# Elementwise work moved from GpSimd to VectorE and ScalarE, and 1024-column modulation products, in a kernel of two transformer blocks

## The chip, the cores and the metric

One core of a Trainium2 chip runs the whole program. The metric is the device time of one execution in microseconds (us): the median of three runs of the kernel before is 2305.88 us. In the profile PE is TensorE's matmul, PEld its weight load, DVE is VectorE, ACT ScalarE, POOL GpSimd and SP SyncE, whose queue issues nearly all DMAs.

## What is computed

Two networks of two layers each are run one after the other on x, 256 tokens by 1024 features, all in float32. The first is a pre-norm block, the second is modulated by rows that come from a condition c (`w_ada`):

```
for l in range(DEPTH):                       # first block
    h = rmsnorm(x, ffn1_pre_g[l])
    x = x + 0.5 * rmsnorm(swiglu(h, ...), ffn1_post_g[l])
    m = hybrid_mixer(rmsnorm(x, mix_pre_g[l]), w_in[l], w_out[l], ...)
    ...
for l in range(DEPTH):                       # second block
    mod = silu(c) @ w_ada[l] + b_ada[l]      # 1024 x 9216, split in nine rows sh, sc, g
    y = _swiglu(_modulate(x, sh1, sc1), ...)
    x = _post_norm(x, y, g1, FFN_RES, ln_gain[l, 0], ln_bias[l, 0])
    y = _token_mixer(_modulate(x, sh2, sc2), w_in[l], w_out[l])
    ...
```

Each layer is a feed-forward net (inner width 2816), a mixer and a second feed-forward net. The mixer of the first block has four parts (gated delta-net, differential attention, state-space, mLSTM), that of the second three (retention, dilated attention, stick-breaking). Several parts end with a norm over each head: `rmsnorm(o, norm_g)`.

## The kernel before, in words

**Weights.** All products run in TensorE's fast float32 format, with three products per pair to keep precision: each weight is split into a high part H, its rounded copy, and a low part L, the rest. The method `unit` (line 768) does it for 128 x 1024 elements: SyncE loads a raw buffer (tiles `raw`, or `rawx` in the SBUF cells R and S), ScalarE casts it to H (`wH`), and L = raw - H is one subtraction (`wL`). Line 783 chooses the engine of the subtraction: of the units counted in `nunit`, every 5th in a feed-forward net (`POOL_FFN`) and every 2nd elsewhere (`POOL_MIX`) goes to GpSimd, the others to VectorE. Some units of a feed-forward net have other buffers, which the profile names by their cells (X, A). The raw buffer comes free when the subtraction has read it. A feed-forward net has 70 units, the first block's mixer 38, the second's 32.

**Stages.** `ffn` (line 919) streams gate and up units through TensorE in column blocks of 512, applies silu on ScalarE, and splits the product into H and L (tiles A and B); `down` (line 995) streams the down weights into accumulators `pa` and `pb`. Then `post_rms` or `post_ln` norms each half of the tokens (`t` is 0 or 1), and the next stage's `pre_rms` or `modulate` norms, scales and transposes the rows (tiles `h` and G, `tr`, `hT`). The reciprocal root of each norm is a power on GpSimd (`pow_rs`, line 763). The mixers weave the projections (`pj`) with the parts' own small products (`pg`, `po`).

**Modulation rows.** `ada_pieces` (line 1036) is a generator: `unit` draws pieces of it at 0.58 per unit while a feed-forward net runs, from the first block's first net to the second block's first. A piece loads two blocks of 128 weight rows by 512 columns and adds them, times the condition's column, into `aacc` (one buffer of 512 columns). After four pieces the sum over partitions is left to do: `aacc` is split into `aaH` and `aaL`, and `ada_row` (line 1064), two pieces later, multiplies them by ones on TensorE, adds the bias and stores the row.

**Head norms.** `head_norm` (line 1132) squares its rows by a product of the tile with itself, on GpSimd unless told otherwise, then reduces on VectorE.

**Order.** Every operation is recorded, not issued; so nearly all have line 637 in the profile, and groups are told apart by tiles. `Program.emit` (line 516) then gives each tile its place (`rooms`: SBUF cells A, B, X, R, S, G, E, L of set widths, E being 568 columns that only mixer tiles use), links operations that share data, and places them by rank on one timeline per engine and one for the wire, each at a duration that `taken` (line 564) estimates. The program is emitted in the order of the planned starts, so each engine works through its own queue in that order. For GpSimd the estimate is

```
occ = 0.05 + (0.0023 if len(ins) > 1 else 0.0011) * n
```

with n columns, and no term for other engines' work.

Of the kernel before, what the change touches and what calls it, by code (L numbers as in the profile page):

```python
# [12 lines left out]
F32 = mybir.dt.float32  # L13
F32R = mybir.dt.float32r
AF = mybir.ActivationFunctionType
ALU = mybir.AluOpType
# [4 lines left out]
P = 128  # L21
D = 1024
S = 256
DFF = 2816
KD = D // P
# [9 lines left out]
NRL = 4  # L35
NLOC = 2
KA = 12
POOL_FFN = 5
POOL_MIX = 2
STAG = 6  # L40
LAST = 2
AHEAD = 12.0
# [2 lines left out]
HALVES = [slice(0, 512), slice(512, 1024)]  # L45
# [550 lines left out]

CELLS = {"A": 6144, "B": 5120, "X": 4096, "R": 2048, "S": 2048, "G": 1536, "E": 568, "L": 4992}
ROOMS = {F32: ("G", "E", "R", "S", "A", "B"), F32R: ("X",)}  # L600
row = lambda c, n, size=1024, at=0: [(c, at + i * size) for i in range(n)]
PLANS = {
    "ffn": {"aA": row("A", 1), "aB": row("B", 1), "wLx": row("X", 2), "wHx": row("X", 2, at=2048),
# [75 lines left out]
class Kern:  # L679
    def __init__(self, ctx, tc, a, out):  # L680
        self.ctx, self.tc, self.a, self.out = ctx, tc, a, out
        self.clock = Clock()
        self.prog = Program(tc)
        self.nc = Engines(self.prog, self.clock)
        self.last_table = None
        self.nffn = 0
        self.done, self.local, self.table_end = [], None, 0.0
        self.nraw, self.nunit, self.ada_gen, self.ada_rate, self.ada_due = 0, 0, iter(()), 0.0, 0.0

    nbufs = {"pa": 4, "pb": 2, "pj": 2, "pg": 2, "po": 2, "tr": 2}  # L690

# [76 lines left out]
    def unit(self, src, a, n):  # L768

        nc, w = self.nc, a * n  # L770
        where = next(self.local) if self.local else ""
        raw = self.raw()
        if where == "a":
            H, L = next(self.late)
        else:
            pool, nb = (self.lp, NLOC) if where else (self.wp, NW)
            L = self.tl(pool, [P, UNIT], "wL" + where, F32R, bufs=nb)
            H = self.tl(pool, [P, UNIT], "wH" + where, F32R, bufs=nb)
        v = lambda t: t[:, :w].rearrange("p (a n) -> p a n", a=a)
        nc.sync.dma_start(v(raw), src.rearrange("(a p) n -> p a n", p=P))  # L780
        nc.scalar.copy(H[:, :w], raw[:, :w])
        self.nunit += 1
        pooled = self.nunit % (POOL_FFN if self.local else POOL_MIX) == 0
        self.sub(L[:, :w], raw[:, :w], H[:, :w].bitcast(F32), nc.gpsimd if pooled else nc.vector)
        if self.local and ADA_FROM <= next(self.count) < ADA_TO:
            self.ada_due += self.ada_rate
        while self.ada_due >= 1:
            self.ada_due -= 1
            next(self.ada_gen, None)
        return v(H), v(L)  # L790
# [244 lines left out]

    def ada_pieces(self):

        nc, last = self.nc, None
        for l in range(LAYERS):
            for j in range(18):  # L1040
                c0 = j * 512
                acc = self.tl(self.adap, [P, 512], "aacc")
                for k0 in range(0, KD, 2):
                    rv = self.raw().rearrange("p (a n) -> p a n", a=2)
                    nc.sync.dma_start(rv, self.a["w_ada_2"][l, k0 * P:(k0 + 2) * P, c0:c0 + 512]
                                      .rearrange("(a p) n -> p a n", p=P))
                    for k in (k0, k0 + 1):
                        cc = self.cond[:, k:k + 1]
                        if k == 0:
                            self.ts(acc, rv[:, 0], cc, None, ALU.mult)  # L1050
                        else:
                            self.stt(acc, rv[:, k - k0], cc, acc, ALU.mult, ALU.add)
                    if k0 == 2 and last:
                        self.ada_row(*last)
                    if k0 + 2 < KD:
                        yield
                H, L = (self.tl(self.adap, [P, 512], n, F32R) for n in ("aaH", "aaL"))
                nc.scalar.copy(H, acc)
                self.sub(L, acc, H.bitcast(F32))
                last = (l, j, H, L)  # L1060
                yield
        self.ada_row(*last)

    def ada_row(self, l, j, H, L):
        nc, c0, m = self.nc, j * 512, j // 2
        row = self.tl(self.adap, [1, 512], "arow", bufs=1)
        nc.sync.dma_start(row, self.a["b_ada_2"][l:l + 1, c0:c0 + 512])
        ps = self.tl(self.trp, [P, 512], "tr")
        self.mm(ps[0:1], self.onesr, H, True, False)
        self.mm(ps[0:1], self.onesr, L, False, True)  # L1070
        self.add(row, row, ps[0:1])
        if m % 3 == 1:
            self.ts(row, row, 1.0, None, ALU.add)
        elif m % 3 == 2:
            self.ts(row, row, 1.0, 1.0 if m == 5 else 0.5, ALU.add, ALU.mult)
        nc.sync.dma_start(self.mods[l, c0:c0 + 512].unsqueeze(0), row)
        self.mods_done = l * 18 + j + 1
# [51 lines left out]
        self.sub(o[:, :, 0], o[:, :, 0], tmp[:, :, 1])  # L1129
        self.add(o[:, :, 1], o[:, :, 1], tmp[:, :, 0])  # L1130

    def head_norm(self, pool, o, n, w, gate, out, tag, eng=None):

        g = lambda ap: ap.rearrange("p (n w) -> p n w", n=n)
        sq = self.tl(pool, [P, n * w], "nsq", bufs=2)
        ss = self.tl(self.sm, [P, n], tag + "ss", bufs=2)
        self.mul(sq, o, o, eng or self.nc.gpsimd)
        self.nc.vector.tensor_reduce(ss, g(sq), AX.X, ALU.add)
        self.ts(ss, ss, 1.0 / w, EPS, ALU.mult, ALU.add)
        self.pow_rs(ss, ss)  # L1140
        if gate is None:
            self.mul(g(out), g(o), self.bc(ss, w))
            return
        self.mul(g(sq), g(o), self.bc(ss, w))
        self.mul(out, sq, gate)
# [288 lines left out]
    def gdn(self, l, m, GP, trp, T, r4, r8):  # L1434
        nc = self.nc
        V, A, G = nc.vector, nc.scalar, nc.gpsimd
        sp = self.sp1[l]
# [3 lines left out]
        E = {}  # L1441
# [191 lines left out]
        def end():  # L1633
            for t in range(2):
                yield f"gscan{t}"
                o = E["o", t]
                self.head_norm(m, o, 4, 64, None, o, "gn", V if t else G)
                self.mul(r4(o), r4(o), self.bm(sp["gdn_norm_g"], 4))
                yield 0.0
            for t in range(2):  # L1640
                yield f"gg{t}"
                self.mul(E["o", t], E["o", t], T["zg", t][:, 256:512])
                self.out_T(E["o", t], 0, t)
# [3 lines left out]
    def diff(self, l, m, OP, trp, T, r4):  # L1647
        nc = self.nc
        V, A, G = nc.vector, nc.scalar, nc.gpsimd
        sp = self.sp1[l]  # L1650
# [9 lines left out]
        for t in range(2):  # L1660
# [41 lines left out]
            o = tl([P, 256], "ho", 8)  # L1702
            A.copy(o, ps[:, 0:256])
            self.head_norm(m, o, 4, 64, None, o, "dn")
            self.mul(r4(o), r4(o), self.bm(sp["diff_norm_g"], 4), G)
            self.out_T(o, 2, t)
        self.flag("diff")

# [303 lines left out]
    def block2(self):  # L2012
        a = self.a
        with ExitStack() as ctx:
            cp = self.pool("con2p", 1, ctx)
            self.rows = self.pool("rows2", 5, ctx)
            self.con2 = self.tl(cp, [P, C2_ARR.shape[1]], "con2")
            self.nc.scalar.dma_start(self.con2, a["con2"])
            self.ada_rate = ADA_RATE
            steps = [(w, l, j) for l in range(LAYERS) for j, w in enumerate(("ffn1", "mix", "ffn2"))]  # L2020
            for (what, l, j), nxt in zip(steps, steps[1:] + [None]):
                r = {}

                def rows():
                    r["g"] = self.mod_row(l, 3 * j + 2)
                    r["gain"], r["bias"] = (self.rowb(a[n][l, j]) for n in ("ln_gain_2", "ln_bias_2"))
                    if nxt is not None:

                        r["scale"], r["shift"] = (self.mod_row(nxt[1], 3 * nxt[2] + q) for q in (1, 0))
                        b = self.tl(self.sc, [P, D], "h")  # L2030
                        self.mul(b, r["bias"], r["scale"], self.nc.gpsimd)
                        self.add(r["shift"], r["shift"], b, self.nc.gpsimd)
                        self.mul(r["scale"], r["scale"], r["gain"], self.nc.gpsimd)

                def tail(t, acc, trp):
                    yield from self.post_ln(t, acc, r, trp)

                if what == "mix":
                    self.mixer2(l, rows, tail)
                else:  # L2040
                    self.ffn(a[what + "_w_gate_2"][l], a[what + "_w_up_2"][l], a[what + "_w_down_2"][l], rows, tail, NRL - 2)
# [181 lines left out]
    def stick(self, m, GP, T, r4):  # L2223
# [16 lines left out]
        yield from self.scores_T(GP, T["sT"], each)  # L2240
        mk = self.bm(self.c2("mlt"), 4)
        for s in range(2):
            self.mul(sp[s][:, :, 0:P], sp[s][:, :, 0:P], mk, G if s else V)
        yield 0.0
        for s in range(2):
            for t in range(s, 2):
# [6 lines left out]
                yield 0.0  # L2253
        for s in range(2):
            self.act(zs[s], zs[s], AF.Exp)
            self.mul(zs[s][:, :, 0:P], zs[s][:, :, 0:P], mk, G if s else V)
        yield "sv1"
        yield 0.0
        for t in range(2):
# [63 lines left out]
```

## Time and profile before

| | us |
|---|---|
| runs shown | 2313.62, 2301.46, 2305.88 |
| median | 2305.88 |
| profiled execution | 2308.43 |
| its span in the profile | 2306.7 |

The profiled execution lies 2.5 us over the median; 1.7 us of it lie around the span. The feed-forward nets and mixers follow each other. In the profile the first mixer lies from about 210 to 430 us, the second from 830 to 1060, the second block's two from 1457 to 1597 and from 1974 to 2116; the rest are the eight feed-forward nets, of 180 to 210 us each. Busy time counts an instruction from its start to its end, whatever it does in between. A wait is idle time of an engine, put down to what ended it.

### The profile page before, as it was taken

The numbers are of one execution on the slowest core, as the hardware profiler recorded it, in microseconds if no ns is written. First come the engines' busy times: TensorE is split into PE (matmuls) and PEld (weight loads), VectorE is DVE, ScalarE is ACT, GpSimd is POOL, SyncE is SP. The second block draws the span as 40 slices with busy tenths as digits, with TensorE's granted clock in tenths as the row PEclk, the third lists the DMA queues.
The fourth block names the chain that finished last, engine by engine and source line by source line (L and its number), as shares of the span: only waits on it lengthen the run. The fifth ranks groups of instructions, "written<-read, shape, count | busy, mean of one in ns | idle before, by whom it ended". The sixth has DMA issues, their size and how long they took to land.

```text
span 2306.7 us, 36694 instructions
## 1 busy us (share of the span) xinstructions
PE 2180.5 (95%) x14604; PEld 1935.7 (84%) x14604; DVE 1641.6 (71%) x2232; ACT 1003.0 (43%) x1420; POOL 570.6 (25%) x292
## 2 busy tenths in 40 slices
PE   8998999999899989999998999998999999998998
PEld 6986888799689868888986898876998898876996
DVE  6788797787788878877777785757645645757544
ACT  5443443544343445335433445343443445344441
POOL 1212323211121232232111132334311222333211
PEclk9999999999899989999999999999999999999999
DMA  9877422687777854136776767436755656435652
GB/s 321 267 268 224 131 74 82 226 278 243 250 255 252 272 182 129 56 127 228 256 253 233 259 213 242 153 119 194 227 191 179 208 155 227 145 111 197 209 189 72
DMA packets 226747, 455.32 MB, mean 197 GB/s; under 512 B 20808, under 2 KB 56008, under 8 KB 226576
## 3 DMA queue, kind: packets, MB, share of 16 engines
q1 hardware_dynamic: 226288, 451.87, 60.2%
q8 instruction: 114, 1.87, 0.3%
q10 hardware_dynamic: 288, 1.11, 0.1%
q14 instruction: 57, 0.47, 0.1%
HBM read 451.80 MB, written 1.12 MB: 196 GB/s over the span
## 4 chain that ended last, share of the span: by engine, by line
PE 62%; DVE 19%; DMA 9%; issue 6%; ACT 3%; POOL 1%; SPq 0%; DVEq 0%; ACTq 0%; POOLq 0%
PE pa L637 38%; PE pj L637 9%; PE pb L637 5%; PE pg L637 4%; DVE aacc L637 4%; PE po L637 3%; DVE wL L637 3%; DVE A L637 3%; PE tr L637 2%; DVE B L637 2%; DVE G L637 2%; DMA raw<-in_ffn_w_down_dram 1%; DMA raw<-in_ffn_w_up_dram 1%; DVE h L637 1%; DVE X L637 1%
## 5 line engine op out<-in xcount | busy, mean ns | idle before, releaser
L637 PE MATMUL pa<-hT,wH 128*128 128x256 f32 x3008 | 546.5, 283 | 0.0
L637 ACT CAST wH<-raw 128x1024 fp32r<-128x1024 f32 (+2 forms) x374 | 375.4, 1013 | 392.2 <-PE pa L637 141.2
L637 POOL TENSOR_TENSOR wL<-raw,wH 128x1024 fp32r<-128x1024 f32 (+1 forms) x120 | 307.6, 2563 | 702.5 <-ACT wH L637 649.9
L637 PEld LDWEIGHTS pa<-hT,wH 128*128 128x128 f32 x3008 | 469.3, 191 | 2.9 <-issue 1.7
L637 DVE TENSOR_TENSOR wL<-raw,wH 128x1024 fp32r<-128x1024 f32 (+2 forms) x254 | 329.4, 1300 | 173.4 <-ACT wH L637 173.2
L637 PE MATMUL pa<-hT,wL 128*128 128x256 f32 x1504 | 425.8, 283 | 0.0
L637 PE MATMUL pa<-hT,X 128*128 128x256 f32 x2400 | 298.7, 279 | 4.2 <-ACT X L637 3.1
L637 PEld LDWEIGHTS pa<-hT,X 128*128 128x128 f32 x2400 | 288.2, 190 | 6.8 <-ACT X L637 3.3
L637 PEld LDWEIGHTS pa<-hT,wL 128*128 128x128 f32 x1504 | 288.2, 192 | 0.0
L637 PE MATMUL pj<-wH,hT 128*128 128x256 f32 (+1 forms) x768 | 207.0, 348 | 0.5 <-ACT hT L637 0.5
L637 PEld LDWEIGHTS pj<-wH,hT 128*128 128x128 f32 x768 | 137.4, 198 | 21.8 <-issue 4.1
L637 DVE TENSOR_TENSOR wL<-R,wH 128x1024 fp32r<-128x1024 f32 (+1 forms) x88 | 113.2, 1289 | 57.3 <-ACT wH L637 57.2
L637 PE MATMUL pa<-wH,hT 128*128 128x512 f32 x384 | 137.4, 417 | 9.9 <-ACT wH L637 4.5
L637 ACT CAST wH<-R 128x1024 fp32r<-128x1024 f32 (+1 forms) x102 | 100.8, 992 | 92.4 <-PE pa L637 39.0
L637 ACT CAST X<-raw 128x1024 fp32r<-128x1024 f32 (+1 forms) x100 | 98.5, 986 | 93.7 <-PE pa L637 56.5
L637 DVE TENSOR_TENSOR X<-raw,X 128x1024 fp32r<-128x1024 f32 (+1 forms) x77 | 96.1, 1248 | 58.1 <-ACT X L637 57.7
L637 POOL TENSOR_TENSOR X<-raw,X 128x1024 fp32r<-128x1024 f32 (+1 forms) x23 | 57.1, 2485 | 323.3 <-ACT X L637 266.1
L637 PE MATMUL pj<-hT,wH 128*128 128x256 f32 (+1 forms) x672 | 131.3, 295 | 0.0
L637 PE MATMUL pj<-wL,hT 128*128 128x256 f32 (+1 forms) x384 | 129.5, 337 | 0.7 <-POOL wL L637 0.5
L637 DVE SCALAR_TENSOR_TENSOR aacc<-raw,cols,aacc 128x512 f32<-128x512 f32 x132 | 115.3, 873 | 12.2 <-DMA raw<-in_w_ada_dram 9.4
L637 PEld LDWEIGHTS pj<-hT,wH 128*128 128x128 f32 (+1 forms) x672 | 105.6, 192 | 3.8 <-issue 0.7
L637 PE MATMUL pb<-wH,A 128*128 128x512 f32 x288 | 103.0, 399 | 1.5 <-ACT wH L637 1.5
(402 smaller groups left out, 3977.7 us busy)
## 6 DMA issues: line engine op xcount, KB each, us to landing
raw<-in_ffn_w_gate_dram SPq DMA_DIRECT2D x111, 512.0 KB
raw<-in_ffn_w_down_dram SPq DMA_DIRECT2D x110, 512.0 KB
raw<-in_w_in_dram SPq DMA_DIRECT2D x108, 512.0 KB
raw<-in_ffn_w_up_dram SPq DMA_DIRECT2D x86, 512.0 KB
raw<-in_w_ada_dram SPq DMA_DIRECT2D x76, 512.0 KB
R<-in_ffn_w_up_dram SPq DMA_DIRECT2D x57, 512.0 KB
R<-in_ffn_w_down_dram SPq DMA_DIRECT2D x48, 512.0 KB
R<-in_w_ada_dram SPq DMA_DIRECT2D x40, 512.0 KB
```

Of the source, the lines that this page charges most:

```text
L637: getattr(self.prog.tc.nc, self.eng).__getattribute__(name)(*[real(x) for x in a], **{q: real(x) for q, x in k.items()})
```

## The change

Subtractions of weights go to VectorE, all of them. So do the product with `diff_norm_g`, the scale and shift rows of the second block (`rows` in `block2`), and the mask products of `stick`. The squares of `head_norm` go to ScalarE. Modulation products take 1024 columns and one block of 128 weight rows per load; `aacc` has 1024 columns and is split in two halves, one after the other. The cell E is dropped. The powers of `pow_rs` and some memsets stay on GpSimd.

```diff
-POOL_FFN = 5
-POOL_MIX = 2
...
-CELLS = {"A": 6144, "B": 5120, "X": 4096, "R": 2048, "S": 2048, "G": 1536, "E": 568, "L": 4992}
-ROOMS = {F32: ("G", "E", "R", "S", "A", "B"), F32R: ("X",)}
+CELLS = {"A": 6144, "B": 5120, "X": 4096, "R": 2048, "S": 2048, "G": 1536, "L": 4992}
+ROOMS = {F32: ("G", "R", "S", "A", "B"), F32R: ("X",)}
...
         nc.scalar.copy(H[:, :w], raw[:, :w])
-        self.nunit += 1
-        pooled = self.nunit % (POOL_FFN if self.local else POOL_MIX) == 0
-        self.sub(L[:, :w], raw[:, :w], H[:, :w].bitcast(F32), nc.gpsimd if pooled else nc.vector)
+        self.sub(L[:, :w], raw[:, :w], H[:, :w].bitcast(F32))
...
-            for j in range(18):
-                c0 = j * 512
-                acc = self.tl(self.adap, [P, 512], "aacc")
-                for k0 in range(0, KD, 2):
-                    rv = self.raw().rearrange("p (a n) -> p a n", a=2)
-                    nc.sync.dma_start(rv, self.a["w_ada_2"][l, k0 * P:(k0 + 2) * P, c0:c0 + 512]
-                                      .rearrange("(a p) n -> p a n", p=P))
-                    for k in (k0, k0 + 1):
-                        cc = self.cond[:, k:k + 1]
...
-                    if k0 == 2 and last:
-                        self.ada_row(*last)
-                    if k0 + 2 < KD:
+            for m in range(9):
+                acc = self.tl(self.adap, [P, D], "aacc")
+                for k in range(KD):
+                    rv = self.raw()
+                    nc.sync.dma_start(rv, self.a["w_ada_2"][l, k * P:(k + 1) * P, m * D:(m + 1) * D])
+                    cc = self.cond[:, k:k + 1]
+                    if k == 0:
+                        self.ts(acc, rv, cc, None, ALU.mult)
+                    else:
+                        self.stt(acc, rv, cc, acc, ALU.mult, ALU.add)
+                    if k == 3 and last:
+                        self.ada_row(*last.pop())
+                    if k < KD - 1:
                         yield
...
+                for n, c in enumerate(HALVES):
+                    if last:
+                        self.ada_row(*last.pop())
+                    H, L = (self.tl(self.adap, [P, 512], q, F32R) for q in ("aaH", "aaL"))
+                    nc.scalar.copy(H, acc[:, c])
+                    self.sub(L, acc[:, c], H.bitcast(F32))
+                    last.append((l, 2 * m + n, H, L))
                 yield
...
-    def head_norm(self, pool, o, n, w, gate, out, tag, eng=None):
+    def head_norm(self, pool, o, n, w, gate, out, tag):
...
-        self.mul(sq, o, o, eng or self.nc.gpsimd)
+        self.nc.scalar.activation(sq, o, AF.Square)
...
-                self.head_norm(m, o, 4, 64, None, o, "gn", V if t else G)
+                self.head_norm(m, o, 4, 64, None, o, "gn")
...
-            self.mul(r4(o), r4(o), self.bm(sp["diff_norm_g"], 4), G)
+            self.mul(r4(o), r4(o), self.bm(sp["diff_norm_g"], 4))
...
-                        self.mul(b, r["bias"], r["scale"], self.nc.gpsimd)
-                        self.add(r["shift"], r["shift"], b, self.nc.gpsimd)
-                        self.mul(r["scale"], r["scale"], r["gain"], self.nc.gpsimd)
+                        self.mul(b, r["bias"], r["scale"])
+                        self.add(r["shift"], r["shift"], b)
+                        self.mul(r["scale"], r["scale"], r["gain"])
...
-            self.mul(sp[s][:, :, 0:P], sp[s][:, :, 0:P], mk, G if s else V)
+            self.mul(sp[s][:, :, 0:P], sp[s][:, :, 0:P], mk)
...
-            self.mul(zs[s][:, :, 0:P], zs[s][:, :, 0:P], mk, G if s else V)
+            self.mul(zs[s][:, :, 0:P], zs[s][:, :, 0:P], mk)
```

## Rows read from the trace of the kernel before

**Rows 1.** The page, part 1: busy us (share of the span) xinstructions of each engine.

```profile
PE 2180.5 (95%) x14604; PEld 1935.7 (84%) x14604; DVE 1641.6 (71%) x2232; ACT 1003.0 (43%) x1420; POOL 570.6 (25%) x292
```

**Rows 2.** Windows: stretch, length, busy us (x) of PE, PEld, DVE, ACT, POOL, clock, DMA.

```profile
220.00:420.00 200.00, 182.84 (x1580) 161.02 (x1580) 160.08 (x350) 85.80 (x168) 62.92 (x40) 0.96 0.37 112
...
1475.00:1584.00 109.00, 104.96 (x583) 85.54 (x579) 68.94 (x108) 52.22 (x83) 50.18 (x22) 1.00 0.46 151
...
1602.00:1778.00 176.00, 176.00 (x1180) 162.43 (x1181) 96.73 (x93) 80.74 (x91) 42.40 (x18) 0.98 0.64 201
```

**Rows 3.** PE's waits, whole span: us in total, times, longest us.

```profile
PE tr L637 <- DVE h L637: 36.9, 11, 11.2
PE tr L637 <- DVE G L637: 15.7, 11, 4.3
PE pg L637 <- DVE A L637: 10.9, 23, 1.6
PE tr L637 <- DVE X L637: 7.2, 4, 1.9
PE tr L637 <- DVE S L637: 6.8, 6, 2.0
...
PE pb L637 <- DVE wL L637: 2.3, 3, 0.8
...
PE pa L637 <- POOL wL L637: 1.4, 1, 1.4
```

**Rows 4.** Timeline of DVE, 820 to 846 us: start us, us, engine, operation.

```profile
827.29 1.20 DVE L637 TENSOR_TENSOR wL<-raw,wH 128x1024 fp32r<-128x1024 f32 x1
...
832.36 3.48 DVE L637 SCALAR_TENSOR_TENSOR x<-h,rr,x 128x512 f32<-128x512 f32 x2 [0.44 <-POOL rr L637]
...
838.69 3.48 DVE L637 SCALAR_TENSOR_TENSOR h<-x,rr,L 128x512 f32<-128x512 f32 x2 [0.44 <-POOL rr L637]
```

**Rows 5.** Timeline of DVE, 620 to 632 us.

```profile
630.26 1.42 DVE L637 SCALAR_TENSOR_TENSOR h<-x,rr,L 128x512 f32<-128x512 f32 x2 [0.66 <-POOL rr L637]
```

**Rows 6.** Timeline of POOL, 820 to 846 us.

```profile
832.29 2.34 POOL L637 TENSOR_TENSOR wL<-raw,wH 128x1024 fp32r<-128x1024 f32 x1
...
838.63 2.34 POOL L637 TENSOR_TENSOR wL<-raw,wH 128x1024 fp32r<-128x1024 f32 x1
```

**Rows 7.** Groups by form, DVE: shapes xcount | busy us, mean ns | idle before.

```profile
L637 DVE TENSOR_TENSOR wL<-raw,wH 128x1024 fp32r<-128x1024 f32 x228 | 311.0, 1367 | 139.4 <-ACT wH L637 139.3
L637 DVE SCALAR_TENSOR_TENSOR aacc<-raw,cols,aacc 128x512 f32<-128x512 f32 x132 | 115.3, 873 | 12.2 <-DMA raw<-in_w_ada_dram 9.4
...
L637 DVE SCALAR_TENSOR_TENSOR x<-x,rr,L 128x1024 f32<-128x1024 f32 x4 | 5.1, 1275 | 0.0
```

**Rows 8.** Groups by form, POOL.

```profile
L637 POOL TENSOR_TENSOR wL<-raw,wH 128x1024 fp32r<-128x1024 f32 x117 | 302.8, 2588 | 688.2 <-ACT wH L637 635.6 <-DVE aaL L637 18.2 <-DVE B L637 14.2
...
L637 POOL TENSOR_TENSOR S<-S,L 128x1024 f32<-128x1024 f32 x4 | 10.9, 2738 | 0.1
...
L637 POOL TENSOR_TENSOR B<-B,L 128x512 f32<-128x512 f32 x4 | 7.0, 1748 | 13.4 <-ACT B L637 9.8 <-DVE B L637 3.6
...
L637 POOL TENSOR_TENSOR G<-G 128x256 f32<-128x256 f32 x4 | 2.7, 672 | 16.9 <-ACT G L637 11.6 <-DVE G L637 5.2
```

**Rows 9.** The waits of DVE, 220 to 420 us.

```profile
DVE wL L637 <- ACT wH L637: 4.5, 2, 2.6
```

**Rows 10.** The waits of DVE, 1475 to 1584 us.

```profile
DVE wL L637 <- ACT wH L637: 9.4, 5, 2.8
...
DVE h L637 <- POOL S L637: 5.0, 1, 5.0
```

**Rows 11.** The chain that ended last, 220 to 420 us, shares by line.

```profile
by line: PE pj L637 19.5%; DVE A L637 12.3%; PE po L637 11.5%; PE pg L637 8.7%; issue 8.1%; DVE B L637 7.8%; DVE S L637 6.9%; DVE wL L637 4.8%; DVE G L637 4.2%; DVE E L637 3.1%; POOL wL L637 2.7%; PE tr L637 2.4%; DMA raw<-in_w_in_dram 2.2%
```

**Rows 12.** The waits of SyncE's DMA queue, whole span.

```profile
SPq L637 <- POOL wL L637: 473.3, 114, 16.0
```

**Rows 13.** Groups by form, ACT.

```profile
L637 ACT ACTIVATE B<-B 128x256 f32<-128x256 f32 x12 | 5.0, 419 | 0.3
```

More of the change, by code (lines that the diff above doesn't have):

```diff
@@ L687, in __init__ @@
         self.done, self.local, self.table_end = [], None, 0.0
-        self.nraw, self.nunit, self.ada_gen, self.ada_rate, self.ada_due = 0, 0, iter(()), 0.0, 0.0
+        self.nraw, self.ada_gen, self.ada_rate, self.ada_due = 0, iter(()), 0.0, 0.0
     nbufs = {"pa": 4, "pb": 2, "pj": 2, "pg": 2, "po": 2, "tr": 2}
@@ L1036, in ada_pieces @@
     def ada_pieces(self):
-        nc, last = self.nc, None
+        nc, last = self.nc, []
         for l in range(LAYERS):
-            for j in range(18):
-                c0 = j * 512
-                acc = self.tl(self.adap, [P, 512], "aacc")
-                for k0 in range(0, KD, 2):
-                    rv = self.raw().rearrange("p (a n) -> p a n", a=2)
-                    nc.sync.dma_start(rv, self.a["w_ada_2"][l, k0 * P:(k0 + 2) * P, c0:c0 + 512]
-                                      .rearrange("(a p) n -> p a n", p=P))
-                    for k in (k0, k0 + 1):
-                        cc = self.cond[:, k:k + 1]
[L1049 to L1052, printed above, removed]
-                    if k0 == 2 and last:
-                        self.ada_row(*last)
-                    if k0 + 2 < KD:
-                        yield
[L1057 to L1060, printed above, removed]
@@ L1061, in ada_pieces @@
                 yield
-        self.ada_row(*last)
+        self.ada_row(*last.pop())
     def ada_row(self, l, j, H, L):
         nc, c0, m = self.nc, j * 512, j // 2
-        row = self.tl(self.adap, [1, 512], "arow", bufs=1)
+        row = self.tl(self.adap, [1, 512], "arow")
         nc.sync.dma_start(row, self.a["b_ada_2"][l:l + 1, c0:c0 + 512])
```

## The prediction

> **What bounds the kernel now.** I read the page's busy line first. TensorE (PE) is busy 2180.5 us of a span of 2306.7 us [rows 1], so at most 126 us of the span is PE standing idle, and the rest moves only if PE's own work gets smaller, which this change does not touch. The stretches confirm it: in a feed-forward stretch of the second block PE is busy for all 176 us, while VectorE (DVE) has work for 96.73 us [rows 2]. The mixers are different: from 220 to 420 us PE is busy 182.84 of 200 us and DVE 160.08, and from 1475 to 1584 us PE is busy 104.96 of 109 [rows 2]. So whatever DVE and GpSimd do counts only where PE waits for them: in the mixers, and at the joints between stages, where a row norm has to end before the next transposes and products.
>
> The waits view names those places. PE's longest waits are all for DVE: 36.9 and 15.7 us for the normed rows `h` and `G` ahead of the transposes, 10.9 us in the delta-net scan, 7.2 and 6.8 us for two more transpose inputs: 77.5 us in five rows [rows 3]. PE waited for a conversion made by GpSimd 1.4 us in the largest row of that kind, and by DVE 2.3 us [rows 3]: the conversions are ahead of PE nearly everywhere, so their own speed is not the point.
>
> What is the point stands in the timelines of the joint near 830 us. There DVE applies a row norm in two instructions of 512 columns, twice: 3.48 us each pair [rows 4]. The same pair near 630 us takes 1.42 us [rows 5]. The difference is what GpSimd does: near 830 us it starts a 2.34 us conversion just after handing over the norm's reciprocal root, at 832.29 and again at 838.63 [rows 6], and DVE's pair, begun at 832.36 and 838.69, cannot get going until it is over; near 630 us no conversion runs. The loss is 3.48 - 1.42 = 2.06 us per pair, almost the length of GpSimd's instruction. So a DVE instruction with two SBUF operands and a GpSimd one exclude each other here, and DVE's blocked time is booked as busy. The average shows it too: the conversion on DVE lasts 1.20 us undisturbed [rows 4], but 1.367 us in the mean over 228 [rows 7], which is 38 us of blocking in that form alone.
>
> The planner that writes the order has no term for this: it prices a GpSimd subtraction at 0.05 + 0.0023 us per column and lets it run beside DVE. So it puts conversions on GpSimd exactly where DVE's work is urgent.
>
> **The change part by part**, against PE's waits.
>
> (a) *182 conversions leave GpSimd.* By the code every 5th of 8 x 70 feed-forward units (112) and every 2nd of 76 + 64 mixer units (70). The blocks they cause go. How much of the 77.5 us is blocking? Near 830 us two pairs lose 2 x 2.06 = 4.1 us ahead of the transposes, and PE's longest wait there, 11.2 us [rows 3], is this one: 37%. Near 630 us nothing is lost and PE waits all the same. I take a quarter of 77.5 us: **-20 us**. Bounds: nothing, if each blocked instruction had slack, to -39 us, if half were blocking (more than the one joint with the most shows).
>
> (b) *The same 182 arrive on DVE*, at 1.20 us each [rows 4] in place of 2.588 [rows 8]: 182 x 1.20 = 218 us of DVE work (less for the dozen of 512 columns). In the feed-forward stretches it lies beside PE's stream: 14 per stretch, 17 us, where even the fullest has slack, and it comes against the blocking that goes. If that cover were gone it would cost those 17 us each. PE's own wait for DVE conversions is 2.3 us in the row shown [rows 3], for some 500 of them; 182 more in proportion are +1 us, and the 1.4 us for GpSimd's [rows 3] goes: together **0**.
>
> (c) *A new wait on DVE's queue.* A conversion waits there for its ScalarE cast, and the scan or the norm behind it waits as well; on GpSimd only conversions stood behind it. In the mixers DVE already waits for casts: 4.5 us between 220 and 420 us [rows 9], 9.4 us between 1475 and 1584 us [rows 10], for the half of the units that it has. As many again are 2 x 4.5 + 2 x 9.4 = 28 us. In the first kind of mixer DVE's lines A, B, S, wL, G and E hold 39% of the chain [rows 11]; 0.39 of 9 us is 4 us; in the second kind PE is nearly full and I count 1 us. **+5 us**; bounds 0 and +28.
>
> (d) *SyncE's queue.* A raw buffer comes free when the subtraction has read it; SyncE waited 473.3 us for GpSimd's [rows 12]. The faster engine frees it 1.4 us sooner, so the weight loads start earlier; bytes stay equal. PE has no long wait for loads behind it: **0**, at best a gain of the few microseconds by which casts come sooner.
>
> (e) *w_ada.* 252 multiply-adds of 512 columns (mean 0.873 us [rows 7]) become 126 of 1024 columns. The nearest row of that shape lasts 1.275 us [rows 7]: 220 us become 161. That is up to 59 us of DVE relief, part of it blocking already counted, all within stretches that PE fills: **0** on the path. The accumulator is one buffer of 1024 columns, split as two halves through one pair of `aaH`/`aaL`, so the next row block waits for a second cast, subtraction and pair of products; the pieces are spread over whole stages, so this hides under PE's stream. Without that cover it would cost about 0.6 + 0.7 us and two products for each of 18 blocks, some 30 us at worst.
>
> (f) *Small operations.* 16 squares go to ScalarE at 0.419 us [rows 13], 14 of them from GpSimd at 0.672 [rows 8]; they stand between a mixer's last sums and its output product: 14 x 0.25 = 3.5 us at most, **-2**. Four mask products leave GpSimd (1.748 us [rows 8]) for DVE at about half that (estimate: the conversion's 1.20 us for twice the columns): **-1**. Fifteen products and sums of scale and shift rows (2.738 us [rows 8]) go to DVE at about 1.2: DVE waited 5.0 us for them in one mixer [rows 10], mostly behind a PE that had work: **-1**.
>
> (g) *The room E goes*, 568 columns of SBUF; small mixer tiles are packed into the rest, so some wait for a predecessor's last reader. No row shows the price. Lower end 0; upper end 5 us per mixer, the size of the one long wait for rows [rows 10], +20 in all; a gain isn't excluded, since the planner redoes the whole order. I take **0**.
>
> Sum: -20 + 0 + 5 + 0 + 0 - 2 - 1 - 1 + 0 = **-19 us**. The profiled execution took 2308.43 us (span 2306.7), 2.5 us over the median of the runs, 2305.88; I take the difference off the median: **2287 us**, 0.8% faster.
>
> The Trainium skill bears on (a): *SBUF — State Buffer*, section "Who interferes with whom", says that DVE and GpSimd share a port pair as an exclusive lock, and that issue order decides who is blocked, for the whole instruction. By that rule alone each conversion could hold DVE up for its whole length, 182 x 2.59 = 471 us (an estimate from that section and this case's duration); the five rows of PE's waits hold 77.5 us, so most of it meets no urgent work. The trace agrees with the mechanism at 832 us.
>
> **The rivals.**
>
> *R1, more is gained.* The norms sit in series, and every joint holds two tiles of rows, so blocks could stack as they do near 830 us. If half of PE's 77.5 us goes, and the waits' other rows shrink in step with a better-timed plan, -39 - 15: about 2252 us. For: the largest wait is 37% blocking. Against: near 630 us there is none. Chance 0.14.
>
> *R2, no change that can be told.* The blocked instructions have slack, or what they give back is taken by (c): -20 x 0.5 + 8 = -2: about 2303 us. For: PE is busy 95% of the span. Chance 0.24.
>
> *R3, slower: DVE becomes the bound of the first block's two mixers.* Each has 38 units, so 19 conversions more, 19 x 1.20 = 23 us, on a DVE that is busy 160 of 200 us [rows 2] and holds 39% of the chain [rows 11]. It decides if the blocked time in there was slack: then DVE's 40 idle us don't shrink, and each mixer gets 23 us longer. +46 - 20 = +26: 2332 us. Against: part of the 160 us is blocking, which goes as GpSimd's 62.92 us there shrink. A rule that speaks this way is in the Trainium skill, *Perfetto Trace Analysis*, "Optimizing Scalar/DVE Operations": where DVE is saturated, offloading may make sense, even to GpSimd, though the same passage doubts it for this pair of engines. Chance 0.12.
>
> *R4, the packing costs its upper end:* 2287 + 20 + 10 for a stall or two of the scans = 2317 and up; chance 0.04.
>
> That the change fails to do what it says: the reciprocal roots (power) and the memsets stay on GpSimd, so short blocks remain, before and after alike.
>
> **How the numbers follow.** My forecast keeps 0.46. About 0.5% (12 us) is what a measurement here can tell from no change. Forecast and R1 lie under 2294: faster 0.60; R2: same 0.24; R3 and R4: slower 0.16. The range: R1's value is the lower end, 2250, with 0.06 below; upward it takes in R2 and stops at 2318, the upper ends of (c) and (g) against half of (a), leaving 0.14 to R3 above. Most of the forecast itself lies between 2270 and 2297.
>
> **What would show it.** Right: GpSimd's busy time falls from 570 us to under 100 us, the DVE conversion's mean to about 1.21 us, pairs at the joints to 1.42 us, DVE's total about as before in spite of 182 more conversions, and PE's waits for `h` and `G` shrink by a quarter or more. Wrong: DVE's pairs stay at 3.4 us somewhere (another blocker), or DVE is busy over 0.95 of a first-block mixer and PE's waits on lines A, B, S grow there (R3), or waits for DVE behind ScalarE casts in the mixers go over 60 us (c).

## The result, and the profile after

| | us |
|---|---|
| before, median of the runs beside it | 2306.45 |
| after, median of 4 runs | 2228.49 (2226.72 to 2232.75) |
| ratio | 0.9662, 95% interval 0.9632 to 0.9692 |
| span of the profiled execution after | 2224.9 (before 2306.7) |

The change gains 78 us, 3.4%. The forecast was 2287 us with a range from 2250: right in its sign, four times too small.

The busy line of the page after, which answers to [rows 1]:

```profile
PE 2158.3 (97%) x14604; PEld 1917.9 (86%) x14604; DVE 1612.4 (72%) x2291; ACT 1022.8 (46%) x1440; POOL 50.3 (2%) x73
```

GpSimd is empty but for the roots and a few memsets, and VectorE, with 182 conversions more, is busy 29 us less. TensorE is the line to look at. Its idle time went from 2306.7 - 2180.5 = 126.2 us to 2224.9 - 2158.3 = 66.6 us; that is 59.6 us of the span. The other 22.2 us are *busy* time that went away at the same 14604 instructions.

Where it went is plain by stages. Here are the first block's two mixers with the joints ahead of them, from the last product of the net before to the last of the mixer, in the kernel before (windows, columns as in [rows 2]):

```profile
202.00:423.00 221.00, 197.91 (x1643) 173.25 (x1642) 176.22 (x373) 96.70 (x190) 68.80 (x48) 0.95 0.39 117
...
823.00:1051.00 228.00, 203.12 (x1645) 179.03 (x1644) 179.32 (x375) 96.24 (x190) 68.45 (x47) 0.91 0.37 114
```

and in the kernel after:

```profile
200.00:392.00 192.00, 187.66 (x1643) 164.60 (x1641) 162.34 (x383) 99.05 (x197) 11.36 (x18) 1.00 0.41 122
...
787.00:980.00 193.00, 187.70 (x1643) 165.02 (x1641) 163.29 (x384) 97.50 (x195) 11.35 (x18) 1.00 0.41 127
```

They are 29 and 35 us shorter, 64 of the 82 us of the span. TensorE's idle time in them fell from 23 and 25 us to 4 and 5 us, and its busy time by 10 and 15 us. The column before the DMA share goes with the second: the granted clock was 0.95 and 0.91 of the full 2.4 GHz and is 1.00. By the traces' clock records TensorE was busy at the lower level of 1.2 GHz for 20 and 32 us of these stretches before, and for none of them after. One product of 512 columns near 830 us lasts 0.40 us at the one level and 0.78 us at the other. So half of that time, 10 and 16 us, is an estimate of what the level cost; the busy time lost about as much.

The joint near 830 us shows how the two hang together. Before, in steps of 5 us:

```profile
823.00:830.00 7.00, 7.00 (x33) 5.68 (x31) 4.31 (x7) 0.53 (x2) 0.00 (x0) 1.00 0.26 75
830.00:835.00 5.00, 0.35 (x2) 0.00 (x0) 3.65 (x5) 2.72 (x6) 3.30 (x2) 0.81 0.32 98
835.00:840.00 5.00, 0.00 (x0) 0.00 (x0) 3.78 (x7) 2.85 (x7) 2.33 (x2) 0.50 0.70 205
840.00:845.00 5.00, 3.43 (x12) 3.01 (x13) 4.18 (x5) 2.02 (x3) 0.96 (x1) 0.50 0.38 110
845.00:850.00 5.00, 5.00 (x20) 4.00 (x19) 4.58 (x7) 1.63 (x3) 3.48 (x5) 0.82 0.65 184
```

After:

```profile
787.00:792.00 5.00, 5.00 (x24) 4.05 (x23) 3.08 (x7) 2.31 (x5) 0.55 (x1) 1.00 0.41 120
792.00:797.00 5.00, 2.68 (x15) 1.99 (x13) 4.24 (x8) 3.80 (x8) 0.55 (x1) 1.00 0.28 79
797.00:802.00 5.00, 5.00 (x26) 4.12 (x26) 4.93 (x9) 2.80 (x5) 0.59 (x2) 1.00 0.28 74
```

Before, TensorE did all but nothing for 10 us, the clock fell to 0.50, the lower level of 1.2 GHz, and stayed there while TensorE was busy again. After, TensorE is idle for 2.3 us and the clock stays up. The first four transposes behind the wait show what the level costs, before and then after:

```profile
841.57 1.12 PE L637 MATMUL tr<-con,h 128*128 128x128 f32 x4 [11.21 <-DVE h L637]
```

```profile
796.44 0.66 PE L635 MATMUL tr<-con,h 128*128 128x128 f32 x4 [2.32 <-DVE h L635]
```

VectorE at that joint after, and GpSimd beside it, to set against [rows 4, 6]:

```profile
791.76 1.40 DVE L635 SCALAR_TENSOR_TENSOR x<-h,rr,x 128x512 f32<-128x512 f32 x2
793.09 1.21 DVE L635 TENSOR_TENSOR wL<-raw,wH 128x1024 fp32r<-128x1024 f32 x1
...
795.64 1.42 DVE L635 SCALAR_TENSOR_TENSOR h<-x,rr,L 128x512 f32<-128x512 f32 x2 [0.73 <-POOL rr L635]
```

```profile
790.29 0.55 POOL L635 TENSOR_TENSOR rr<-rv,mhalf 128x1 f32<-128x1 f32 x1 [180.23 <-DVE rv L635]
795.05 0.55 POOL L635 TENSOR_TENSOR rr<-rv,mhalf 128x1 f32<-128x1 f32 x1 [4.21 <-DVE rv L635]
```

The pairs take 1.40 and 1.42 us in place of 3.48, and each root 0.55 us. A conversion now stands between them, 1.21 us long, while ScalarE sums the squares.

TensorE's waits after, to set against [rows 3]:

```profile
PE tr L635 <- DVE h L635: 18.0, 8, 8.0
PE tr L635 <- DVE G L635: 11.7, 12, 2.2
...
PE pa L635 <- DVE wL L635: 4.2, 4, 1.3
PE tr L635 <- DVE X L635: 2.9, 2, 1.5
...
PE pg L635 <- DVE A L635: 2.8, 8, 0.4
```

The five rows of 77.5 us are now 35.4 us (that for S is gone). How much of this was blocking they don't say, since the order is new too; the run in the old order below tells them apart. The forms of [rows 7] have lost their excess; the conversion takes its 1.22 us in the mean, and no longer 1.37:

```profile
L635 DVE TENSOR_TENSOR wL<-raw,wH 128x1024 fp32r<-128x1024 f32 x345 | 417.9, 1220 | 115.8 <-ACT wH L635 112.6 <-DMA L<-mods 1.5 <-DMA raw<-in_ffn_w_up_dram 0.6
...
L635 DVE SCALAR_TENSOR_TENSOR aacc<-raw,cols,aacc 128x1024 f32<-128x1024 f32 x66 | 84.5, 1281 | 13.6 <-DMA raw<-in_w_ada_dram 12.7
```

### The profile page after: what moved, and what is told of

Its sections match the earlier page's. It is cut to its first block, busy times and chain, and to the rows that moved or that the text cites. A ratio compares the mean times of both kernels' runs of the same rounds, so it can differ in the third digit from the quotient of the medians.

```text
span 2224.9 us, 36427 instructions
## 1 busy us (share of the span) xinstructions
PE 2158.3 (97%) x14604; PEld 1917.9 (86%) x14604; DVE 1612.4 (72%) x2291; ACT 1022.8 (46%) x1440; POOL 50.3 (2%) x73
## 4 chain that ended last, share of the span: by engine, by line
PE 75%; DVE 12%; DMA 7%; issue 3%; ACT 2%; POOL 1%; SPq 0%; DVEq 0%; ACTq 0%; POOLq 0%
PE pa L635 46%; PE pj L635 12%; PE pb L635 7%; PE po L635 4%; PE pg L635 3%; DVE wL L635 3%; PE tr L635 3%; DVE G L635 1%; DVE A L635 1%; DMA raw<-in_ffn_w_down_dram 1%; DVE aacc L635 1%; DMA arow<-in_b_ada_dram 1%; DVE X L635 1%; DVE h L635 1%; DVE R L635 1%
## 5 line engine op out<-in xcount | busy, mean ns | idle before, releaser
L635 DVE TENSOR_TENSOR wL<-raw,wH 128x1024 fp32r<-128x1024 f32 (+2 forms) x374 | 437.0, 1177 | 148.5 <-ACT wH L635 145.3
L635 PE MATMUL pa<-hT,X 128*128 128x256 f32 x2400 | 307.3, 282 | 0.0
L635 PEld LDWEIGHTS pa<-hT,X 128*128 128x128 f32 x2400 | 296.9, 188 | 2.2 <-issue 0.9
L635 PE MATMUL pj<-wH,hT 128*128 128x256 f32 (+1 forms) x768 | 202.0, 341 | 0.7 <-DVE G L635 0.7
L635 DVE TENSOR_TENSOR X<-raw,X 128x1024 fp32r<-128x1024 f32 (+1 forms) x100 | 114.7, 1147 | 67.6 <-ACT X L635 65.7
L635 PEld LDWEIGHTS pj<-wH,hT 128*128 128x128 f32 x768 | 131.7, 189 | 23.4 <-issue 5.8
L635 PE MATMUL pa<-wH,A 128*128 128x512 f32 x288 | 102.2, 395 | 0.0
L635 PEld LDWEIGHTS pa<-wH,hT 128*128 128x128 f32 x384 | 76.0, 201 | 26.7 <-ACT wH L635 5.9
L635 PE MATMUL pj<-hT,wL 128*128 128x256 f32 (+1 forms) x336 | 94.7, 282 | 0.0
```

Of the source, the lines that this page charges most:

```text
L635: getattr(self.prog.tc.nc, self.eng).__getattribute__(name)(*[real(x) for x in a], **{q: real(x) for q, x in k.items()})
```

## The experiments

All ratios are to the kernel before, run beside each on the same chip; 0.01 is 23 us.

| run | us | ratio (95% interval) |
|---|---|---|
| conversions alone, planned on VectorE | 2247.22 | 0.974 (0.9709 to 0.9771) |
| conversions alone, order as before | 2255.45 | 0.9772 (0.9739 to 0.9806) |
| after, order kept, share run on GpSimd | 2311.80 | 1.0037 (1.0012 to 1.0061) |
| after, share planned and run on GpSimd | 2288.34 | 0.9918 (0.9889 to 0.9946) |
| GpSimd kept in the nets only | 2257.44 | 0.9797 (0.9763 to 0.983) |
| GpSimd kept in the mixers only | 2282.14 | 0.9905 (0.9868 to 0.9942) |
| small operations alone | 2295.86 | 0.9974 (0.9952 to 0.9995) |
| wider w_ada pieces alone, no room E | 2309.86 | 1.004 (1.0019 to 1.006) |
| no room E alone | 2309.18 | 1.0027 (0.9998 to 1.0057) |
| after with the old pieces | 2241.72 | 0.9741 (0.97 to 0.9781) |
| the same with GpSimd reads that nobody uses | 2367.43 | 1.0285 (1.0249 to 1.0322) |
| the same with GpSimd writes that nobody uses | 2279.81 | 0.9913 (0.9882 to 0.9944) |

### Is it the conversions, and is it their place in the order?

The first run changes one line, the second only the engine that carries it out (the plan still prices and places it as GpSimd's):

```diff
-        self.sub(L[:, :w], raw[:, :w], H[:, :w].bitcast(F32), nc.gpsimd if pooled else nc.vector)
+        self.sub(L[:, :w], raw[:, :w], H[:, :w].bitcast(F32))
```

```diff
+        self.swap = Engine("vector", "pool", clock, prog)
...
-        self.sub(L[:, :w], raw[:, :w], H[:, :w].bitcast(F32), nc.gpsimd if pooled else nc.vector)
+        self.sub(L[:, :w], raw[:, :w], H[:, :w].bitcast(F32), nc.swap if pooled else nc.vector)
```

> The kernel before with all 182 weight subtractions on VectorE, planned and run there; squares, masks, rows, w_ada pieces and room E as before. Theory P (port: the gain is the end of GpSimd's conversions excluding VectorE's two-operand instructions): most of the 78 us, 2235 to 2260 us. Rival A (the gain is mostly w_ada's wider pieces and the small operations): 2285 to 2306 us.

> The kernel before, its order planned as before (the 182 subtractions still priced and placed as GpSimd work), but run on VectorE. TensorE's instruction order is that of before. Theory P: the exclusion is gone, so most of what the conversions bring comes without a new order: 2240 to 2275 us. Rival O (the new order is what gains, because the planner now knows that the conversions take VectorE's time): VectorE is loaded as the plan does not expect, 2295 to 2330 us.

Measured: 0.974 and 0.9772, 60 and 53 us. So the conversions hold three quarters of the gain, and nearly all of that comes with TensorE's order unchanged. A better plan may add some 7 us (the two intervals overlap). Rivals A and O fall.

The second run shows what the end of GpSimd's conversions is worth by itself. Its busy line, its first transposes at the joint that was near 830 us, and TensorE's waits:

```profile
PE 2153.8 (95%) x14604; PEld 1917.0 (85%) x14604; DVE 1640.8 (73%) x2414; ACT 1007.2 (45%) x1420; POOL 110.0 (5%) x110
```

```profile
808.68 0.66 PE L637 MATMUL tr<-con,h 128*128 128x128 f32 x4 [2.52 <-DVE h L637]
```

```profile
PE tr L637 <- DVE h L637: 24.2, 9, 8.2
PE tr L637 <- DVE G L637: 21.9, 13, 5.4
PE pg L637 <- DVE A L637: 10.4, 22, 1.3
PE tr L637 <- DVE X L637: 4.9, 2, 2.7
...
PE tr L637 <- DVE S L637: 0.5, 2, 0.2
```

At that joint the wait fell from 11.2 to 2.5 us in an unchanged order, by twice the 4.1 us that the two pairs of [rows 4] had lost. The norm's chain up to the transposes is 2.9 us shorter: the 4.1 us, less what two conversions that now stand in it take. For the other 5.8 us VectorE used to come late to the joint, against TensorE's products. Two of its instructions ahead, at 799.63 and 813.48, took 2.64 and 2.72 us beside conversions on GpSimd, where their like take 0.48 and 1.22; that is 3.7 us of it. Over the whole span the five rows fell by less, from 77.5 to 61.9 us. TensorE's idle time fell by 24.4 us (2255.5 - 2153.8 = 101.7 us are left) and its busy time by 26.7 us.

The reverse, on the changed kernel: its order with GpSimd carrying out every 5th and every 2nd conversion, and a plan made anew for that (the same with `nc.gpsimd` in place of `nc.swap`).

```diff
+        self.swap = Engine("gpsimd", "dve", clock, prog)
...
-        self.sub(L[:, :w], raw[:, :w], H[:, :w].bitcast(F32))
+        self.nunit += 1
+        pooled = self.nunit % (5 if self.local else 2) == 0
+        self.sub(L[:, :w], raw[:, :w], H[:, :w].bitcast(F32), nc.swap if pooled else nc.vector)
```

> The changed kernel, its order planned as changed, but every 5th subtraction of a feed-forward net and every 2nd of a mixer run on GpSimd at the places planned for VectorE. TensorE's order is that of the changed kernel. Theory P: the exclusion is back, 2275 to 2320 us. Rival O: the good order keeps most of its gain, 2228 to 2250 us.

> The changed kernel with the share of the subtractions back on GpSimd, planned and run there (every 5th and every 2nd); everything else as changed. Theory P: 2285 to 2310 us, as if only the small parts of the change were left. Rival A: 2228 to 2250 us.

Measured: 1.0037 and 0.9918. With the conversions back on GpSimd the rest of the change is worth 0.8% at best, and in an order made for VectorE it is all lost.

### Is it the exclusion, or GpSimd's late results?

Nothing uses the results of these two runs' extra work; only a few of ScalarE's casts wait for it, 5 to 7 us in total, because GpSimd still has their buffer in hand. The base is the changed kernel with the old w_ada pieces (SBUF for the scratch tile comes from there); the lines run inside the cast's emission, so every other engine's order stays.

```diff
-        nc.scalar.copy(H[:, :w], raw[:, :w])
+        cast = nc.scalar.copy(H[:, :w], raw[:, :w])
...
+                first()
...
+                for q in range(w // 512):
+                    g.tensor_tensor(a4(z), a4(h[:, q * 512:(q + 1) * 512]), one.unsqueeze(1).to_broadcast([P, 4, P]), ALU.subtract)
...
+                g.tensor_tensor(z[:, 0:1], h[:, 0:1], one[:, 0:1], ALU.subtract)
+                for q in range(w // 256):
+                    g.memset(z, 0.0)
```

> The changed kernel with the w_ada pieces of before (512 columns at a time), room E still gone. Also the base for the two runs after it. If the wider pieces are hidden under TensorE's stream, as the prediction had it: 2222 to 2238 us. Rival A (the wider pieces give what the subtractions do not): 2240 to 2252 us.

> The kernel of the run before it, with extra work on GpSimd that nobody waits for: behind the cast of every 5th unit of a feed-forward net and every 2nd of a mixer, two subtractions of 512 columns from H into a scratch tile. Emitted outside the plan: every other engine's order stays word for word. Theory P (exclusion): VectorE is held up as before the change, 40 to 75 us over the base. Rival L (GpSimd's subtractions cost because their results come late): nothing is late here, within 8 us of the base.

> As the run before, but the extra work only writes: one subtraction of one column from H and four memsets of the scratch tile, about as long together. GpSimd is as busy and the roots of the norms queue behind it as long. Theory P, in the form that GpSimd's reads exclude VectorE's second operand: within 15 us of the base, what it has from the queued roots. Rival Q (what costs is the queue on GpSimd ahead of the roots, or any GpSimd traffic): as slow as the run with reads, 40 to 75 us over the base.

Measured: 2241.72 for the base (above the range of the prediction; the last section of experiments comes back to it), 125.7 us more with reads, 38.1 us more with writes. Neither increment lies in a range that was written down: reads cost more than the 40 to 75 us of theory P, writes more than its 15 us, and rival Q had both alike. Rival L, with 8 us for the reads, falls as the sole cause. The conversion's form (groups by form, VectorE), with reads and then with writes:

```profile
L635 DVE TENSOR_TENSOR wL<-raw,wH 128x1024 fp32r<-128x1024 f32 x345 | 490.9, 1434 | 77.9 <-ACT wH L635 76.4 <-DMA raw<-in_ffn_w_up_dram 0.6
```

```profile
L635 DVE TENSOR_TENSOR wL<-raw,wH 128x1024 fp32r<-128x1024 f32 x345 | 417.7, 1219 | 120.0 <-ACT wH L635 119.1
```

GpSimd's writes leave VectorE's instruction at 1.219 us, its reads stretch it to 1.434. The Trainium skill says so too (*SBUF — State Buffer*, "Who interferes with whom": two SBUF inputs contend with a GpSimd instruction that reads SBUF, not with one that only writes it); the two rows agree. What the writes cost instead is the queue ahead of the roots. VectorE's waits for them, base and then writes:

```profile
DVE x L635 <- POOL rr L635: 4.6, 8, 0.7
...
DVE h L635 <- POOL rr L635: 2.3, 4, 0.7
```

```profile
DVE x L635 <- POOL rr L635: 10.9, 10, 3.8
DVE h L635 <- POOL rr L635: 9.3, 6, 3.8
```

The longest grew from 0.7 to 3.8 us. So both theories hold a part here: a busy GpSimd delays the roots (38 us with the writes), and reads come on top (125.7 - 38.1 = 88 us). With reads GpSimd is busy longer, 705 us against 561, but the roots are no later for it: VectorE's waits for them are 11.9 and 8.5 us in the same two rows. The 88 us aren't the queue. This is more reading than the change took away, 653 us of GpSimd's time against some 450 us of conversions before.

In the kernel before, the plan knew GpSimd's work, and the roots didn't queue:

```profile
DVE h L637 <- POOL rr L637: 3.6, 6, 0.7
DVE x L637 <- POOL rr L637: 3.3, 6, 0.7
```

After the change these rows are 2.9 and 4.1 us. So a queue ahead of the roots can cost as much as 38 us, but the change had none to take away.

### Where are the conversions dear?

```diff
-POOL_MIX = 2
+POOL_MIX = 1 << 20
```

(the first run; the second has `POOL_FFN = 1 << 20`).

> The kernel before with GpSimd's subtractions kept in the feed-forward nets (112) and moved to VectorE in the mixers (70). Theory P with the two traces' stages (the first block's mixers with their joints lost some 60 us): most of the 60 us of all subtractions, 2255 to 2270 us. Rival F (the 62% that lie in the feed-forward nets hold 62% of the gain): 2278 to 2290 us.

> The kernel before with GpSimd's subtractions kept in the mixers (70) and moved to VectorE in the feed-forward nets (112). Theory P: 2285 to 2300 us. Rival F: 2262 to 2275 us.

Measured: 47 us from the 70 conversions of the mixers, 22 us from the 112 of the nets: 0.67 and 0.20 us each. Together 69 us, a little over the 60 of all at once. Theory P's range holds for the first; the second lies just under it, and Rival F's ranges miss both. In the nets TensorE streams, so what is saved there should lie at the joints; this is argued, not measured.

### The rest: small operations, w_ada and room E

The edits are parts of the change's diff on the kernel before: the first its lines on `head_norm`, `diff_norm_g`, the rows of `block2` and the masks, as in

```diff
-        self.mul(sq, o, o, eng or self.nc.gpsimd)
+        self.nc.scalar.activation(sq, o, AF.Square)
```

the second its `ada_pieces` and `ada_row` with the lines below, the third these alone:

```diff
-CELLS = {"A": 6144, "B": 5120, "X": 4096, "R": 2048, "S": 2048, "G": 1536, "E": 568, "L": 4992}
-ROOMS = {F32: ("G", "E", "R", "S", "A", "B"), F32R: ("X",)}
+CELLS = {"A": 6144, "B": 5120, "X": 4096, "R": 2048, "S": 2048, "G": 1536, "L": 4992}
+ROOMS = {F32: ("G", "R", "S", "A", "B"), F32R: ("X",)}
```

> The kernel before with the small operations alone moved: squares of head norms to ScalarE; the product with diff_norm_g, the rows of block 2 and the masks to VectorE. The prediction's sum for these: -4 us, so 2298 to 2306 us. If they are what the subtractions leave open: 2285 to 2294 us.

> The kernel before with the w_ada pieces of 1024 columns alone, and room E gone to make place; GpSimd keeps its work. If the wider pieces gain by themselves, as the two runs with and without them say of the changed kernel (13 to 18 us): 2286 to 2297 us. If the prediction's 0 holds, or E's loss takes it: 2298 to 2312 us.

> The kernel before without room E, nothing else. The prediction's term: 0, at most +20 us: 2300 to 2326 us. If the room is worth nothing: within 6 us of before.

Measured: -6 us for the small operations (forecast -4; the median of 2295.86 lies under the range written, the ratio is what counts); w_ada's wider pieces with the loss of E, +9 us; the loss of E alone, +6 us, an interval that reaches to no change. So before, the wider pieces bring nothing. With GpSimd empty the base above is slower than the changed kernel, and four runs side by side settle how (the third is the base with E back, the fourth the changed kernel with `"E": 200` in the SBUF left over):

> The changed kernel, again, beside the three runs after it on the same chip: 0.962 to 0.970 of before.

> The changed kernel with w_ada pieces of 512 columns, room E gone, again. Theory W (without GpSimd's subtractions the wider pieces do gain, since VectorE's time is then what the plan says): 0.5% to 0.9% over the changed kernel. Rival N (the first difference was chips and plan luck): within 0.3%.

> The changed kernel with w_ada pieces of 512 columns and room E of 568 columns kept: all but the wider pieces. If room E is worth nothing here: as the run before it, within 0.3%. If the packing costs, as without the change (0.3%): 0.3% to 0.6% under it.

> The changed kernel with a room E of 200 columns in the SBUF that it leaves unused. If the packing costs something: up to 0.4% under the changed kernel; if not, within 0.2% of it.

| run | us | ratio (95% interval) |
|---|---|---|
| after, again | 2228.78 | 0.9664 (0.9629 to 0.9699) |
| after, old pieces, no E | 2243.05 | 0.9716 (0.9682 to 0.9749) |
| after, old pieces, E kept | 2229.46 | 0.9669 (0.9635 to 0.9704) |
| after, E of 200 columns | 2224.95 | 0.9642 (0.9607 to 0.9676) |

Losing E costs 14 us (2243.05 against 2229.46; no run without it is as fast as the slowest with it), and the wider pieces earn 14 us back (2228.78): together nothing. The simpler kernel with the old pieces and E equals the changed one, so the subtractions and the small operations give the whole 78 us. Each alone they gave 60 and 6; the 12 us between are about what the intervals leave open. A room of 200 columns takes another 4 us off; its four runs reach from 2221.36 to 2227.9 against 2226.86 to 2235.26, but the ratios' intervals overlap. Its median is the lowest here.

E's 14 us aren't waits. With E TensorE is busy 2147.1 us and idle 79.8, without it 2170.3 and 76.2. The largest part shows in a group of products in the nets, with E and then without:

```profile
L635 PE MATMUL pa<-hT,X 128*128 128x256 f32 x2400 | 295.5, 278 | 2.4 <-ACT X L635 2.4
```

```profile
L635 PE MATMUL pa<-hT,X 128*128 128x256 f32 x2400 | 307.7, 282 | 0.3 <-DVE X L635 0.2
```

The kernel before and the one that only lacks E differ alike there, 298.7 and 311.4 us. Why the room's absence slows products of the nets, which keep nothing in it, no run shows.

## Why the prediction was wrong

Its mechanism was right. Conversions on GpSimd hold up VectorE's two-operand instructions, in the mixers and at the joints, and GpSimd's time, the pairs' 1.42 us, the conversion's 1.22 us and VectorE's total, near what it was, all came as said. Its size was wrong, and one sentence of it with the size.

*"The rest moves only if PE's own work gets smaller, which this change does not touch."* This is the step that failed. It fixed the ceiling and put every term in the currency of TensorE's waits, and it is false: the same 14604 matmuls took 22.2 us less after the change, and 26.7 us less with the conversions alone in the order of before, where that is half of the gain. TensorE's busy time holds stretches at 1.2 GHz, in and behind its waits. By the clock records it was busy at that level for 100 us before, 55 us with the conversions alone in the old order, and 29 us after. If half of this time is the price of the level, by the 0.40 and 0.78 us of one product, 50 us of loss became 27 and 14. That is a gain of 23 and 36 us to which the prediction gave no term; of the 36 the missing room E took 14 back. With that price taken off, the seven kernels with the full room E are busy 2124 to 2133 us and the ten without it 2141 to 2151, whatever their waits; so the clock accounts for the busy time but for E's part. This is worked out from the traces; no run changed the clock and left the waits.

*Term (a), mis-sized.* It took 37% of the longest wait for blocking, from the two pairs that show it. With the order unchanged 78% of that wait went (11.2 to 2.5 us), because what is lost ahead of a joint is carried into it. Over the whole span the five rows then fell by 15.6 us and all idle time by 24.4 us, close to the 20 us forecast; that closeness is partly luck, since the share behind it was half of the measured one. The term as a whole measured 53 us in the old order, because the clock came on top.

*The new order had no term.* From there to the changed kernel idle time falls by another 35.1 us, to 66.6 us. Rival R1 alone had a better-timed plan. It put 54 us on waits that go, and 59.6 us of idle time went; its 2252 us lack the busy time.

*Term (c), +5 us, did not come.* VectorE's waits for casts, summed over the whole span, were, before and then after:

```profile
DVE wL L637 <- ACT wH L637: 244.9, 145, 5.0
DVE X L637 <- ACT X L637: 105.6, 71, 5.3
```

```profile
DVE wL L635 <- ACT wH L635: 209.6, 186, 4.1
DVE X L635 <- ACT X L635: 115.5, 105, 3.8
```

350.5 us became 325.1 although 182 conversions joined the queue. The new order isn't the reason: in the order of before, with the conversions on VectorE, the two rows are 246.1 and 104.4 us, 350.5 in sum again. In the first mixer's stretch the row for `wL` went from 4.5 to 3.2 us, where the term had it double. With it falls R3: VectorE is busy 162 of 192 us in the first mixer stretch after, and TensorE's idle time there is 4 us, so VectorE did not become its bound.

*The other terms.* (b) held: TensorE's waits for `wL` are 4.2 us in their largest row. (d) stays open: ScalarE's waits for weight loads into `raw`, R and S fell from 313 to 263 us with the conversions on VectorE in the old order, so buffers that come free sooner may hold a part of the 53 us; no run tried that by itself. (f) said -4 and measured -6. (e) and (g) were both put at 0 and are -14 and +14 with GpSimd empty; the sum was right by accident, and (g) for another reason than mixer tiles that wait. R2's slack was not there: the order of before gains 53 us from the other engine alone. And where the prediction expected short blocks from GpSimd's memsets, the run with writes shows none on the conversion.

## What to carry to other kernels

Work moved to GpSimd isn't free beside VectorE: a subtraction that takes 2.6 us there, with SBUF operands, stops VectorE's two-operand instructions, and a planner without that term can put it where VectorE's work is urgent, as near 830 us. Compare one instruction's mean with its undisturbed duration, and look at what GpSimd does under each long one, before counting it as VectorE's own time. And price a wait of TensorE at more than its length: the matmuls behind it may run at the lower clock, which the page books as busy.

## What the runs showed of the hardware

That the clock follows waits as short as these was not expected: at the joint near 830 us it was 0.81, 0.50, 0.50 and 0.82 over 20 us, in and behind a wait of 11.2 us, and without such waits the two mixers are busy 25 us less. Nor that GpSimd's memsets, 2.3 us at a stretch, leave VectorE's subtraction as it is (1219 ns against 1220), where GpSimd's reads add 0.2 us to it in the mean. The second operand needn't be a tile: `aacc<-raw,cols`, one tile times a column, takes 480 ns in the base, 481 beside the writes and 684 beside the reads.
